# A third home for raw down blocks, the residual in DRAM, and an eighth step by seven products

## The chip, the cores and the metric

The kernel runs on one core of one Trainium2 chip. The core's engines are PE (TensorE, the matmuls), DVE (VectorE), ACT (ScalarE), POOL (GpSimd) and SP (SyncE, which only issues transfers here). Each has its own queue and works it in order; they wait for each other by semaphores. The metric is the device time of one execution in microseconds (us).

## The reference

One layer of a hybrid decoder for 256 tokens and 16 meta tokens put ahead of them, in fp32. The model is 2048 wide, the feed-forward part 5632:

```python
u = rmsnorm(h, norm_mix)
# in projection; 8 retention heads and 4 mLSTM heads, each normed and gated
mix = jnp.concatenate([ret, hm], axis=-1) @ w_out
h = h + mix
u = rmsnorm(h, norm_ffn)
up = causal_dwconv(u @ w_up, ffn_conv_w, ffn_conv_b)      # 3 taps, over the tokens
gate, val = jnp.split(up, [FFN_DIM], axis=-1)
h = h + (jax.nn.silu(gate) * val) @ w_down
h = rmsnorm(h, norm_final)
return h[:, N_META:]
```

The change concerns the last product, (silu(gate) * val) @ w_down, and the sum h that it is added to.

## The kernel before

**Numbers in two parts.** A weight block comes from DRAM as fp32 into a tile `wraw` (4 buffers). ACT casts it to `whi`, DVE subtracts to get the rest `wlo` (5 buffers each, `load_w`, L118 to L123). The left operands are held in two parts as well (`uh`/`ul`, `mh`/`ml`, `sh`/`sl`). A product is then three matmuls: whi by the high part, whi by the low part, wlo by the high part.

**Stages.** In projection and heads (to about 383 us), out projection (to 470), then twice (for each half of the 5632 columns): the up projection with convolution and gate (470 to 718, 828 to 1084), and the down projection in two passes, b=0 (the left 1024 of the 2048 output columns) and b=2 (the right 1024): 718 to 773 and 773 to 828, 1084 to 1140 and 1140 to 1198. The rest is the last norm and the output.

**A down pass** has 11 steps q, each over 256 of the inner columns, for two token tiles tt and two output blocks of 512 (j). A *plain* step does it with `product`: 24 matmuls of 128x512 (L827, L828, L830). A *fast* step (`seven`, L859 to L862) computes the 2x2 block product with seven block products in place of eight, in 21 matmuls. Its left sides (S1 to S4, A11, A12, A22) are made in the up stage. Its right sides are differences and sums of the weight blocks B11, B12, B21, B22; one of these sums is made early, in the out stage or the up stage, by `Early`: POOL loads three blocks into a home, DVE combines them in two operations, and the result is put into DRAM (`kept`). In the down step SP loads the kept sum and three raw blocks into one of two homes (`left`, in the old hT), DVE forms `ta` (L844, 128x1024) and `tb` (L845, 128x512) in wraw tiles, and each group is split by ACT and DVE (L764, L766). FAST has seven of the eleven steps; in the last pass the last two of them (BOTH) are plain.

**PSUM.** A pass uses eight banks: four `cs[tt, j]` (tile atps) and four `ps` (mmps) for the products that are shared. After the last fast step, `share` turns the four into sums and adds them to the residual; at the end of the pass ACT copies the four cs into x tiles (L951), and accumulating transfers (`onto`, L878, by POOL) add these to the residual as well. The next pass starts its matmuls on the same banks.

**The residual** h is transposed in the first up half by 32 DVE operations of 32x512 (`transposed_h`, L675) into `hn` (two token tiles by 2048) in SBUF, where all sums are added.

**The last pass.** Its order of steps is written out. The last four plain steps do only j=0 in their turn; for j=1 they follow `alone`, after the pass, first for token tile 0 in 512 columns, then for token tile 1 in two halves of 256, so that the first tile's norm and output (`finish`: L711 to L727) runs beside the second tile's matmuls. `add` (L900) adds a bank to hn, `squares` (L694) sums the squares on ACT, `gather` (L703, L704) collects them.

**Order.** A scheduler sets the order on each engine from its own model of the times, within the dependencies and the `issue_after` hints in the code.

Of the kernel before, what the change touches and what calls it, by code (L numbers as in the profile page):

```python
# [16 lines left out]
P = 128  # L17
DM = 2048
# [65 lines left out]
def trunk(ctx: ExitStack, tc: tile.TileContext, io, out: bass.AP):  # L84
# [477 lines left out]
    hnp_cm = pool("hnp", 1, side="right")  # L562
    hnp = hnp_cm.__enter__()
    hn = hnp.tile([P, 2, DM], F32, name="hn")
# [7 lines left out]
    ssq = hn[:, 0, 0:NQ]  # L572
# [20 lines left out]
    FAST = [1, 2, 3, 5, 6, 7, 8]  # L593
# [5 lines left out]
    class Early:  # L599


        def __init__(self, b, q, home, after, pace=None):

            self.home, self.age = home, 0
            self.kept = dram.tile([P, 512], F32, name=f"kept{b}_{q % NQD}", bufs=1)
# [6 lines left out]
        def finish(self, after):  # L612
            t = self.home[:, 0, :]
            with tc.issue_after(after.ins):
                nc.vector.tensor_tensor(out=t, in0=self.home[:, 1, :], in1=t, op=ALU.subtract)
            nc.vector.tensor_tensor(out=t, in0=self.home[:, 2, :], in1=t, op=ALU.add)
            nc.gpsimd.dma_start(self.kept, t)

    early, running = {}, []
    ahead = [(0, q) for q in FAST[:5]]  # L620
# [43 lines left out]
    x5 = midp.tile([P, 5, 512], F32, name="x5")  # L664
    pace = midp.tile([P, 1], F32, name="pace")

    def x_tile(i):
        return x5[:, i, :]

    def transposed_h(i, a):  # L670

        src = hT[32 * i : 32 * (i + 1), :, T0 + 2 :].rearrange("p k (t a e) -> p k t a e", t=2, e=32)
        dst = hn[32 * a : 32 * (a + 1), :, :].rearrange("p t (k f) -> p k t f", f=P)
        for t in range(2):
            nc.vector.transpose(dst[:, :, t, 32 * i : 32 * (i + 1)], src[:, :, t, a, :])  # L675

    def conv3(ps, f, name):
# [3 lines left out]
        o = wk2.tile([P, SEQ], F32, name=name)  # L681
# [59 lines left out]
    left = hT.rearrange("p k t -> p (k t)")[:, 0:4096].rearrange("p (i a n) -> i p a n", i=2, a=4)  # L741
    turn = 0

    for half in range(2):
        units = [(b, q) for b in (0, 2) for q in FAST if (half, b) != (1, 2) or q not in BOTH]
        homes = [left[0][:, 0:3, :], left[1][:, 0:3, :], x5[:, 1:4, :]]
        if half == 0:
            units = units[len(ahead):]
            begins = [2 + 4 * i for i in range(9)]
            homes = 9 * [homes[2]]  # L750
# [18 lines left out]
        for jj in range(NHF):  # L769
# [27 lines left out]
            else:  # L797
# [5 lines left out]
                nc.gpsimd.tensor_tensor(out=sums[:, S3, :], in0=e11, in1=e21, op=ALU.subtract)  # L803
# [28 lines left out]
        def seven(b, q, cs, ps, first, last, after, norm):  # L832
# [5 lines left out]
            turn = 1 - turn  # L838

            nc.sync.dma_start(raw[:, 0, :], early[b, q])  # L840
# [4 lines left out]
            nc.vector.tensor_tensor(out=tb[:, 0, :], in0=raw[:, 3, :], in1=raw[:, 0, :], op=ALU.subtract)  # L845
            copied = None
            for w, to in (
                (raw[:, 2:4, :], ((S4, cs[0, 1], False, False), (A12, cs[0, 0], False, False))),
                (raw[:, 0:2, :], ((S2, ps[2], first, last), (A11, ps[0], first, last))),
                (ta, ((S3, ps[1], first, last), (S1, ps[3], first, last))),  # L850
                (tb[:, 0:1, :], ((A22, cs[1, 0], False, False),)),
# [9 lines left out]
                for i, (m, o, _, end) in enumerate(to):  # L861
                    nc.tensor.matmul(o, sh[:, f, m, :], lo[:, i, :], start=False, stop=end)  # L862
            if norm:
# [4 lines left out]
                reached = nc.gpsimd.tensor_tensor(out=junk[:, 0:1], in0=tb[:, 0, 0:1], in1=tb[:, 0, 0:1], op=ALU.add)  # L868
# [4 lines left out]
        def block(tt, b):  # L873
            return hn[:, tt, b * 512 : (b + 1) * 512]
# [194 lines left out]
```

## Time and profile before

| | us |
|---|---|
| median of three runs (lowest, highest) | 1207.89 (1206.9, 1209.06) |
| profiled execution | 1207.7 |
| span of its profile | 1205.9 |
| busy: PE, DVE, ACT, POOL | 1194.6, 971.5, 709.5, 162.8 |
| granted clock of PE | 0.999 |

The profile is one execution. A row of a timeline gives start and duration, then engine, line, operation, what it writes and reads, how many, and in brackets the idle time ahead of it and what ended it. A group's row gives its count, the total busy time and the mean in ns, then the idle time ahead of the group. A row of a stretch gives its bounds, its length, the busy time of each engine, the granted clock, the share of the 16 DMA engines, and GB/s.

### The profile page before, as it was taken

What the parts mean: (1) busy time and instruction counts of PE and PEld (TensorE: products, weight loads), DVE (VectorE), ACT (ScalarE), POOL (GpSimd) and SP (SyncE); (2) the same over time, 40 slices, a digit from 0 to 9 for tenths busy, and PEclk for the clock granted to TensorE, in tenths of its full rate; (3) what the DMA queues carried; (4) which work ended last, traced back from release to release, by engine and by line L of the source; (5) the groups of instructions that cost most, each with busy time, mean ns of one, the idle gap of its engine ahead of it and who ended that gap; (6) DMA issues with size and microseconds to landing.
All of it is one profiled execution on the core that took longest, in us unless ns stands there. A gap on an engine that the chain in (4) does not pass through costs nothing.

```text
span 1205.9 us, 22794 instructions
## 1 busy us (share of the span) xinstructions
PE 1194.6 (99%) x8956; PEld 1151.2 (95%) x8956; DVE 971.5 (81%) x1444; ACT 709.5 (59%) x963; POOL 162.8 (14%) x223
## 2 busy tenths in 40 slices
PE   9999999999999999999999999999999999999997
PEld 9999999999999999999999998878999999998886
DVE  8968788766775966789889879897788778789897
ACT  8747656655656646555555557664555555556664
POOL 0100001111110311021122100202022112100232
PEclk9999999999999999999999999999999999999999
DMA  8765555666565965766766834959787777755956
GB/s 278 269 212 164 170 184 170 197 183 192 169 192 165 349 200 175 252 220 212 253 219 214 279 117 175 278 177 276 284 251 255 223 240 249 261 176 211 274 181 186
DMA packets 83004, 263.27 MB, mean 218 GB/s; under 512 B 14672, under 2 KB 18896, under 8 KB 82768
## 3 DMA queue, kind: packets, MB, share of 16 engines
q1 hardware_dynamic: 71952, 223.85, 57.0%
q0 software_dynamic: 10368, 37.11, 10.1%
q8 instruction: 70, 1.15, 0.4%
q10 hardware_dynamic: 576, 0.85, 0.2%
q14 instruction: 38, 0.31, 0.1%
HBM read 243.42 MB, written 11.27 MB: 211 GB/s over the span
## 4 chain that ended last, share of the span: by engine, by line
PE 96%; DMA 2%; DVE 1%; ACT 0%; issue 0%; SPq 0%; DVEq 0%; ACTq 0%
PE mmps L130 26%; PE mmps L131 25%; PE mmps L133 25%; PE atps L827 2%; PE atps L828 2%; PE atps L830 2%; PE mmps L860 2%; PE mmps L862 2%; PE mmps L859 2%; PE atps L862 1%; PE atps L860 1%; PE atps L859 1%; DMA hn<-x 1%; PE atps L379 1%; DMA hT<-in_wd 1%; PE atps L371 0%
## 5 line engine op out<-in xcount | busy, mean ns | idle before, releaser
L121 ACT CAST whi<-wraw 128x1024 fp32r<-128x1024 f32 x352 | 369.3, 1050 | 342.0 <-PE mmps L131 228.7
L123 DVE TENSOR_TENSOR wlo<-wraw,whi 128x1024 fp32r<-128x1024 f32 x352 | 432.3, 1230 | 72.5 <-ACT whi L121 70.0
L130 PE MATMUL mmps<-uh,whi 128*128 128x258 f32 x1408 | 346.1, 283 | 0.0
L131 PE MATMUL mmps<-ul,whi 128*128 128x258 f32 x1408 | 346.0, 283 | 0.0
L130 PEld LDWEIGHTS mmps<-uh,whi 128*128 128x128 f32 x1408 | 267.6, 190 | 0.1
L131 PEld LDWEIGHTS mmps<-ul,whi 128*128 128x128 f32 x1408 | 267.1, 190 | 0.1
L130 PE MATMUL mmps<-xh,whi 128*128 128x272 f32 (+2 forms) x864 | 219.8, 288 | 0.0
L131 PE MATMUL mmps<-xl,whi 128*128 128x272 f32 (+2 forms) x864 | 218.3, 286 | 0.0
L133 PE MATMUL mmps<-uh,wlo 128*128 128x258 f32 x1408 | 196.5, 282 | 0.0
L133 PEld LDWEIGHTS mmps<-uh,wlo 128*128 128x128 f32 x1408 | 179.9, 189 | 0.0
L131 PEld LDWEIGHTS mmps<-xl,whi 128*128 128x128 f32 x864 | 162.8, 188 | 0.0
L130 PEld LDWEIGHTS mmps<-xh,whi 128*128 128x128 f32 x864 | 162.5, 188 | 0.1
L133 PE MATMUL mmps<-xh,wlo 128*128 128x272 f32 (+2 forms) x864 | 126.7, 285 | 0.0
L133 PEld LDWEIGHTS mmps<-xh,wlo 128*128 128x128 f32 x864 | 114.2, 188 | 0.0
L680 DVE TENSOR_TENSOR cu<-mmps,rstd 128x258 f32<-128x258 f32 x88 | 37.4, 425 | 55.3 <-PE mmps L133 54.8
L764 ACT CAST whi<-hT 128x1024 fp32r<-128x1024 f32 x52 | 53.6, 1052 | 27.2 <-PE atps L828 7.3
L766 DVE TENSOR_TENSOR wlo<-hT,whi 128x1024 fp32r<-128x1024 f32 x52 | 62.1, 1220 | 4.9 <-ACT whi L764 3.7
L131 PE MATMUL mmps<-mixl,whi 128*128 128x258 f32 x256 | 63.0, 283 | 0.0
L130 PE MATMUL mmps<-mixh,whi 128*128 128x258 f32 x256 | 62.4, 282 | 0.0
L764 ACT CAST whi<-wraw 128x1024 fp32r<-128x1024 f32 (+1 forms) x52 | 43.0, 838 | 16.8 <-PE mmps L860 6.8
L766 DVE TENSOR_TENSOR wlo<-wraw,whi 128x1024 fp32r<-128x1024 f32 (+1 forms) x52 | 52.2, 1037 | 0.6 <-PE mmps L862 0.2
L827 PE MATMUL atps<-whi,mh 128*128 128x512 f32 (+1 forms) x132 | 50.9, 387 | 1.3 <-ACT whi L121 1.1
(280 smaller groups left out, 1700.1 us busy)
## 6 DMA issues: line engine op xcount, KB each, us to landing
wraw<-in_wu SPq DMA_DIRECT2D x176, 512.0 KB, 4.4
wraw<-in_wi SPq DMA_DIRECT2D x108, 512.0 KB, 4.1
hT<-in_wd SPq DMA_DIRECT2D x26, 768.0 KB, 4.7
wraw<-in_wd SPq DMA_DIRECT2D x36, 512.0 KB, 4.7
wraw<-in_wo SPq DMA_DIRECT2D x32, 512.0 KB, 4.2
x<-in_wd POOLq DMA_DIRECT2D x13, 768.0 KB, 7.0
hn<-x POOLq DMA_DIRECT2D x27, 256.0 KB, 7.9
hT<-kept SPq DMA_DIRECT2D x26, 256.0 KB, 2.9
```

What stands on the lines that cost most here:

```text
L121: nc.scalar.copy(hi, raw)
L123: nc.vector.tensor_tensor(out=lo, in0=raw, in1=hi.bitcast(F32), op=ALU.subtract)
L130: nc.tensor.matmul(ps, hi[:, k, :], xh(kk), start=kk == first, stop=False)
L131: nc.tensor.matmul(ps, hi[:, k, :], xl(kk), start=False, stop=False)
L133: nc.tensor.matmul(ps, lo[:, k, :], xh(kk), start=False, stop=kk == last)
L680: evacuated = nc.vector.tensor_tensor(out=u, in0=ps[:, :NQ], in1=rstd2, op=ALU.mult)
L764: copied = nc.scalar.copy(hi, x)
L766: return copied, nc.vector.tensor_tensor(out=lo, in0=x, in1=hi.bitcast(F32), op=ALU.subtract)
L827: nc.tensor.matmul(ps, ah[i], hi[:, i, cols], start=first and i == 0, stop=False)
L859: nc.tensor.matmul(o, sh[:, f, m, :], hi[:, i, :], start=begin, stop=False)
L860: nc.tensor.matmul(o, sl[:, f, m, :], hi[:, i, :], start=False, stop=False)
L862: nc.tensor.matmul(o, sh[:, f, m, :], lo[:, i, :], start=False, stop=end)
```

## The change

- FAST gets q=4: eight of eleven steps are fast. In the last pass six are (the steps 7 and 8 stay plain there), and the order of its steps becomes 0, 1, 2, 7, 3, 4, 8, 5, 6, 9, 10.
- Early keeps both of its sums (512 KB) instead of one (256 KB). A fast step then loads 512 KB of sums, 512 KB of raw blocks and 256 KB for B22 into a tile of its own (b22, two buffers), and forms only one difference (ta). The weight layout wd7 and the sign of S3 follow.
- A third home for raw blocks (`third`); the three take turns.
- The out stage makes eight sums early instead of five (four homes `eh`), the first up half eight instead of nine, the second up half fourteen instead of twelve, with four homes.
- The residual no longer stays in SBUF: it is transposed in pieces (128 operations of 32x128) into `third`, four transfers put it into DRAM (`hnd`), and the 16 accumulating transfers of half 0 add to it there. In half 1, b=0, four transfers bring it back (512 KB each, one after each of the first four fast steps), and gfin (1 MB) follows after the fifth.
- There are four x tiles instead of five; ssq lives in rstd2; vt has one buffer.

The core of the diff:

```diff
-    FAST = [1, 2, 3, 5, 6, 7, 8]
+    FAST = [1, 2, 3, 4, 5, 6, 7, 8]
...
-            self.kept = dram.tile([P, 512], F32, name=f"kept{b}_{q % NQD}", bufs=1)
+            self.kept = dram.tile([P, 2, 512], F32, name=f"kept{b}_{q % NQD}", bufs=1)
...
-    homes = 2 * [eh.tile([P, 3, 512], F32, name=f"eh{i}") for i in range(3)]
-    begins = [1, 4, 6, 8, 10]
+    homes = 2 * [eh.tile([P, 3, 512], F32, name=f"eh{i}") for i in range(4)]
+    begins = [0, 2, 3, 5, 7, 8, 10, 12]
...
-    def transposed_h(i, a):
...
+    def transposed_h(g, i):
+        turned = left[2][:, 2 * (g % 2) : 2 * (g % 2) + 2, :]
...
+        for a in range(4):
+            dst = turned[32 * a : 32 * (a + 1), :, :].rearrange("p t (k f) -> p k t f", f=P)
+            for t in range(2):
+                nc.vector.transpose(dst[:, :, t, 32 * i : 32 * (i + 1)], src[:, :, t, a, :])
+        if i == 3:
+            nc.gpsimd.dma_start(hnd[:, :, 512 * g : 512 * (g + 1)], turned)
...
+    left = [left[0], left[1], midp.tile([P, 4, 512], F32, name="third")]
...
             raw = left[turn]
-            turn = 1 - turn
-            nc.sync.dma_start(raw[:, 0, :], early[b, q])
-            nc.sync.dma_start(raw[:, 1:4, :], io["wd7"][b // 2, half * NQD + q][:, 1:4, :])
-            ta, tb = (wpool.tile([P, 2, 512], F32, name="wraw", bufs=4) for _ in range(2))
-            nc.vector.tensor_tensor(out=ta, in0=raw[:, 0:1, :].to_broadcast([P, 2, 512]), in1=raw[:, 1:3, :], op=ALU.subtract)
-            nc.vector.tensor_tensor(out=tb[:, 0, :], in0=raw[:, 3, :], in1=raw[:, 0, :], op=ALU.subtract)
+            turn = (turn + 1) % 3
+            w = io["wd7"][b // 2, half * NQD + q]
+            nc.sync.dma_start(raw[:, 0:2, :], early[b, q])
+            nc.sync.dma_start(raw[:, 2:4, :], w[:, 2:4, :])
+            b22 = midp.tile([P, 1, 512], F32, name="b22", bufs=2)
+            nc.sync.dma_start(b22[:, 0, :], w[:, 1, :])
+            ta = wpool.tile([P, 2, 512], F32, name="wraw", bufs=4)
+            nc.vector.tensor_tensor(out=ta, in0=raw[:, 2:4, :], in1=raw[:, 1:2, :].to_broadcast([P, 2, 512]), op=ALU.subtract)
...
+            if half == 1 and b == 0 and fast.index(q) < 5:
+                refill(fast.index(q), copied)
...
         def block(tt, b):
-            return hn[:, tt, b * 512 : (b + 1) * 512]
+            return (hn if half == 1 else hnd)[:, tt, b * 512 : (b + 1) * 512]
...
-            steps = [0, 1, 4, 2, 7, 3, 5, 6, 8, 9, 10] if final else range(NQD)
+            steps = [0, 1, 2, 7, 3, 4, 8, 5, 6, 9, 10] if final else range(NQD)
...
-                        x = x_tile((4, 3, 1, 0)[2 * j + n])
+                        x = x_tile((3, 1, 0, 2)[2 * j + n])
```

Where the order moves. On SP, at the start of half 0, b=2, the loads before the change are these (kept and hT: the two loads of a fast step; wraw x4: the plain steps' weights):

```order
L840 DMA hT<-kept_1_6644 128x512
L841 DMA hT<-in_wd 128x1536
L118 DMA wraw<-in_wd 128x1024 x2
L840 DMA hT<-kept_2_6936 128x512
L841 DMA hT<-in_wd 128x1536
L118 DMA wraw<-in_wd 128x1024 x4
L840 DMA hT<-kept_3_7228 128x512
L841 DMA hT<-in_wd 128x1536
```

And the same place after it (b_: the tile b22):

```order
L118 DMA wraw<-in_wd 128x1024
L845 DMA third<-in_wd 128x1024
L844 DMA third<-kept_1_6082 128x1024
L847 DMA b_9494<-in_wd 128x512
L118 DMA wraw<-in_wd 128x1024
L845 DMA hT<-in_wd 128x1024
L844 DMA hT<-kept_2_6372 128x1024
L847 DMA b_9670<-in_wd 128x512
L118 DMA wraw<-in_wd 128x1024
L845 DMA hT<-in_wd 128x1024
L844 DMA hT<-kept_3_6676 128x1024
L847 DMA b_9713<-in_wd 128x512
```

Three transfers stand for a fast step where two stood, and the loads of step 3 are issued ahead of the last plain weights instead of behind them. On DVE, at the end of the program, before:

```order
L900 TENSOR_TENSOR hn<-atps,hn 128x512 x2
L703 TENSOR_REDUCE rest<-ss_5848 128x1
L704 TENSOR_SCALAR rest<-rest 128x1
L900 TENSOR_TENSOR hn<-atps,hn 128x512
L711 TENSOR_SCALAR frt<-ss_5848,rest 128x1
L900 TENSOR_TENSOR hn<-atps,hn 128x256
L713 SCALAR_TENSOR_TENSOR frt<-frt,fr_5852 128x1
L714 SCALAR_TENSOR_TENSOR frt<-frt,fr_5852 128x1
L723 TENSOR_SCALAR hn<-hn,frt 128x256
L723 TENSOR_SCALAR hn<-hn,frt 128x768
L721 SCALAR_TENSOR_TENSOR hn<-hn,frt,gfin 128x512
```

And after (the lines are shifted: L907 is `add`, L725 and L723 the scalings of `finish`, L705 and L706 `gather`):

```order
L907 TENSOR_TENSOR hn<-atps,hn 128x512
L706 TENSOR_SCALAR rest<-rest 128x1
L907 TENSOR_TENSOR hn<-atps,hn 128x512
L713 TENSOR_SCALAR frt<-ss_5861,rest 128x1
L715 SCALAR_TENSOR_TENSOR frt<-frt,fr_5865 128x1
L716 SCALAR_TENSOR_TENSOR frt<-frt,fr_5865 128x1
L725 TENSOR_SCALAR hn<-hn,frt 128x256
L725 TENSOR_SCALAR hn<-hn,frt 128x768
L723 SCALAR_TENSOR_TENSOR hn<-hn,frt,gfin 128x512
L907 TENSOR_TENSOR hn<-atps,hn 128x256
L705 TENSOR_REDUCE rest<-ss_5861 128x1
L706 TENSOR_SCALAR rest<-rest 128x1
```

The first sum of 256 columns has moved from ahead of the three scalings to behind them. On PE, the wide matmuls of token tile 0 that follow alone now all stand ahead of the narrow ones of token tile 1; before, the last pair stood among them.

More of the change, by code (lines that the diff above doesn't have):

```diff
@@ L904, in trunk, with refill @@
             up_cm.__exit__(None, None, None)
[L905 removed]
+            more_cm = pool("more", 1, side="right")
             more = more_cm.__enter__()
+            hn = more.tile([P, 2, DM], F32, name="hn", bufs=1)
             gfin = more.tile([P, DM], F32, name="gfin", bufs=1)
[L908 removed]
+            def refill(n, after):
+                cols = slice(n * 512, (n + 1) * 512)
+                with tc.issue_after(after.ins):
+                    if n < 4:
+                        nc.gpsimd.dma_start(hn[:, :, cols], hnd[:, :, cols])
+                    else:
+                        nc.gpsimd.dma_start(gfin, io["gfin"])
             junk = more.tile([P, 512], F32, name="junk", bufs=1)
```

50 lines of the change are left out of this document (21 added, 29 removed).

## The prediction

> **What bounds the kernel now.** I read the page's busy shares first, then the list of what PE (TensorE) waits for, then the four down passes as stretches of time.
>
> ```profile
> span 1205.9 us, 22794 instructions
> PE 1194.6 (99%) x8956; PEld 1151.2 (95%) x8956; DVE 971.5 (81%) x1444; ACT 709.5 (59%) x963; POOL 162.8 (14%) x223
> PE 96%; DMA 2%; DVE 1%; ACT 0%; issue 0%; SPq 0%; DVEq 0%; ACTq 0%
> ```
>
> PE works 1194.6 of 1205.9 us and is 96% of the chain that ended last. A change pays by taking matmuls away or by closing a PE gap; everything on another engine is free as long as PE's next operand is there. The gaps are few:
>
> ```profile
> PE atps L827 <- ACT whi L121: 1.1, 2, 0.7
> PE atps L130 <- ACT whi L224: 0.7, 1, 0.7
> PE atps L827 <- ACT x L951: 0.2, 1, 0.2
> ```
>
> (total us, times, longest). The L827 rows lie in the down passes, the other at the start, untouched. The down passes, in order (half 0 b=0, b=2, half 1 b=0, b=2), then two short stretches:
>
> ```profile
> core 0: us, PE busy (x) PEld busy (x) DVE busy (x) ACT busy (x) POOL busy (x), PEclk, DMA share, GB/s
> 718.00:773.00 55.00, 55.00 (x243) 45.17 (x242) 49.88 (x54) 33.00 (x38) 3.54 (x4) 1.00 0.66 222
> 773.00:828.00 55.00, 53.90 (x234) 43.55 (x234) 50.44 (x52) 34.62 (x41) 6.99 (x8) 1.00 0.69 203
> 1084.50:1140.00 55.50, 55.50 (x243) 45.24 (x241) 50.35 (x55) 34.66 (x40) 4.03 (x5) 1.00 0.73 244
> 1140.00:1197.70 57.70, 57.54 (x274) 47.99 (x273) 52.62 (x58) 36.73 (x54) 19.26 (x18) 1.00 0.61 184
> 1122.00:1128.00 6.00, 6.00 (x28) 4.91 (x27) 5.32 (x6) 2.91 (x4) 0.00 (x0) 1.00 1.03 370
> 410.00:415.00 5.00, 5.00 (x44) 5.00 (x44) 5.00 (x6) 2.25 (x3) 2.67 (x4) 1.00 1.03 412
> ```
>
> PE is full in each pass but the second, which lacks 1.1 us. DVE (VectorE) is over 90% busy there, and the transfers come in bursts: 370 and 412 GB/s are the most that full queues moved.
>
> **Part 1: one more step by seven products.** In four passes one step (4 in three of them; in the last pass six fast steps instead of five) needs 21 matmuls of 128x512 instead of 24: 4 x 3 = 12 fewer. PE starts one every 0.23 us:
>
> ```profile
> 765.73 0.39 PE L828 MATMUL atps<-whi,ml 128*128 128x512 f32 x1
> 765.96 0.39 PE L827 MATMUL atps<-whi,mh 128*128 128x512 f32 x1
> 766.19 0.39 PE L828 MATMUL atps<-whi,ml 128*128 128x512 f32 x1
> ```
>
> 12 x 0.23 = **-2.76 us**, wholly on the path, since PE is the path. A plain step is 24 x 0.23 = 5.5 us, a fast one 21 x 0.23 = 4.8 us.
>
> **Part 2: third home, one wraw tile per fast step.** The two L827 waits:
>
> ```profile
> 793.62 0.50 PE L827 MATMUL atps<-whi,mh 128*128 128x512 f32 x1 [0.45 <-ACT whi L121]
> 819.27 0.51 PE L827 MATMUL atps<-whi,mh 128*128 128x512 f32 x1 [0.65 <-ACT whi L121]
> 788.90 0.93 SPq L118 DMA_DIRECT2D wraw<-in_wd  x2
> 792.52 1.05 ACT L121 CAST whi<-wraw 128x1024 fp32r<-128x1024 f32 x1 [2.94 <-DMA wraw<-in_wd]
> SPq L840 <- DVE wlo L766: 63.4, 11, 13.8
> ```
>
> The weights of plain step 4 are issued only at 788.90, the cast (792.52) waits 2.94 us for them, and PE waits for the cast. SP issues in order: its hT loads wait for a free home (63.4 us in the two passes of half 0), and the four wraw slots hold both differences of each fast step. With three homes, one difference per step, and step 4 no longer plain, both causes shrink. I take both waits as gone: **-1.1 us** (bounds 0 and -1.1).
>
> On DVE the second difference falls away:
>
> ```profile
> L675 DVE STREAM_TRANSPOSE hn<-hT 32x512 f32<-32x512 f32 x32 | 20.7, 681 | 0.2
> L845 DVE TENSOR_TENSOR wraw<-hT 128x512 f32<-128x512 f32 x26 | 17.8, 685 | 0.1
> L336 DVE STREAM_TRANSPOSE turns<-vT 128x256 f32<-128x256 f32 x16 | 7.0, 437 | 0.0
> L337 DVE STREAM_TRANSPOSE turns<-vT 128x32 f32<-128x32 f32 x16 | 2.7, 169 | 0.0
> ```
>
> 26 x 0.685 = 17.8 us less, none of it on the path: DVE stays behind PE in cover. But a fast step still asks DVE for about 5.1 us (today's split and differences, 5.8, less 0.685) against PE's 4.8, so eight in a row eat about 8 x 0.3 = 2.4 us of DVE's lead. The plain steps 9, 10 and 0 give it back, so I price this at nothing.
>
> **Part 3: residual by DRAM.** The 32 transposes become 128 of 32x128. No row shows that shape; by the 128x32 and 128x256 rows one costs 0.17 to 0.44 us, by a straight line 0.28: 128 x 0.28 = 36 us against 20.7, so +15 us (+1 to +35). They run in the first up half, where this row gives the cover:
>
> ```profile
> 475.00:700.00 225.00, 225.00 (x1879) 225.00 (x1878) 192.78 (x295) 122.93 (x165) 39.22 (x55) 1.00 0.71 233
> ```
>
> DVE has 32 us free: nothing on the path; at the upper end 3 us could show. The eight sums of the out stage (five before) bring three loads and larger stores there; that stage had PE full at 412 GB/s, so I price it at 0, with 2 us as the upper bound.
>
> The 16 accumulating transfers of half 0 go to DRAM. Their nearest rows are the same transfers into SBUF:
>
> ```profile
> hn<-x POOLq DMA_DIRECT2D x27, 256.0 KB, 7.9
> 766.03 2.77 POOL L878 DMA_DIRECT2D hn<-x  x3 [1.25 <-DVE x L887]
> 772.92 2.25 ACT L951 COPY x<-atps 128x512 f32<-128x512 f32 x4
> 777.87 0.39 PE L827 MATMUL atps<-whi,mh 128*128 128x512 f32 x1
> ```
>
> The last of the three is issued near 767.6 and lands, by the median of 7.9 us, at 775.5. With one x tile fewer, the fourth copy out of PSUM at the pass boundary now waits for exactly that landing. PE wants this bank at 777.87, the copy takes 0.57: slack 1.8 us. At SBUF's speed this costs nothing; if DRAM takes longer by more than 1.8 us, PE waits. For all new waits together (this landing, a late load) I take one late load of the size seen, **+0.65 us** (0 to +4).
>
> **Part 4: the end.** In the last stretch the scaling of the first token tile now stands on DVE ahead of the first half-block sum, and the third of the four sums of a wide bank (L907 now, L900 before) waits for the last accumulating transfer.
>
> ```profile
> 1180.49 1.05 ACT L121 CAST whi<-wraw 128x1024 fp32r<-128x1024 f32 x1 [2.75 <-DMA wraw<-in_wd]
> 1191.39 0.28 PE L827 MATMUL atps<-whi,a21h 128*128 128x256 f32 x1
> 1192.22 0.63 PE L830 MATMUL atps<-wlo,mh 128*128 128x512 f32 x2
> 1197.30 0.40 PE L830 MATMUL atps<-wlo,mh 128*128 128x256 f32 x2
> 1192.89 0.69 DVE L900 TENSOR_TENSOR hn<-atps,hn 128x512 f32<-128x512 f32 x1 [0.51 <-PE atps L830]
> 1194.88 0.42 DVE L900 TENSOR_TENSOR hn<-atps,hn 128x256 f32<-128x256 f32 x1 [0.24 <-PE atps L830]
> 1195.67 1.43 DVE L723 TENSOR_SCALAR hn<-hn,frt 128x256 f32<-128x256 f32 x2
> 1197.67 0.14 DVE L703 TENSOR_REDUCE rest<-ss 128x1 f32<-128x4 f32 x1
> 1197.92 0.41 DVE L900 TENSOR_TENSOR hn<-atps,hn 128x256 f32<-128x256 f32 x1
> 1198.91 0.21 DVE L711 TENSOR_SCALAR frt<-ss,rest 128x1 f32<-128x1 f32 x1 [0.58 <-ACT junk L694]
> ```
>
> E is PE's end (1197.30 + 0.40 = 1197.70). Today seven narrow matmuls (1191.39 to 1192.22, 0.83 us) stand ahead of the last pair of 512; now all 48 narrow ones follow it, so the sum of 1192.89 can come 0.83 us earlier against E. The three scalings take 1195.67 to 1197.67: 2.00 us. At best they now run from E-2.86 to E-0.86; the first half-sum follows, its square is in 0.99 us later (as 1197.92 to 1198.91), reduce and scale take 0.25 (1197.67 to 1197.92), and the second half-sum starts at E+0.38 instead of E+0.22: +0.16 us. But the last fast step now ends 12 wide matmuls nearer to E (57 before, 45 after), so its sums and their transfers end up to 2.76 us nearer to E, unless the 2.75 us that ACT lost at 1180.49 to a late load come back, which would cancel it. Bounds +0.16 and 0.16 + 2.76 = +2.9; I take **+0.8**, near the lower, because that load is now issued earlier.
>
> **Sum:** -2.76 - 1.10 + 0.65 + 0.80 = -2.4 us. The profiled execution took 1207.7: 1207.7 - 2.4 = 1205.3. It lies 0.2 below the median of the runs, 1207.89, so on that footing 1205.5, a change of -0.2%. Some 0.2% (2.4 us) is about what a measurement of this kernel can tell from no change; the forecast stands on that edge.
>
> **Refill traffic against full queues.** In half 1 b=0 each of five fast steps now asks for 1280 KB of weights and sums (1.31 MB) and four of them for 512 KB of residual as well: 1.83 MB in 4.8 us is 382 GB/s. The rows above show 370 and 412 at full queues, so the four steps need 0.0 to 0.7 us more than PE gives them in all (4 x 1.83 / 370 = 19.8 us against 19.2), which a lookahead of one home, 4.8 us, covers. In the Trainium skill, "DMA: Bandwidth & Descriptors", section "Where 436 GB/s comes from", the HBM side (about 358 GB/s) binds for transfers between HBM and SBUF; by it the steps would need 4 x 1.83 / 358 = 20.4 us, an estimate that adds 0.6 us to the shortage. The trace does not agree: 412 GB/s passed here.
>
> **The rivals.**
> *Everything arrives* (0.25): both waits go, the end costs 0.16 and no new wait comes: 1207.7 - 3.7 = 1204.0, on the median's footing 1204.2. For it: PE waited only 1.3 us in four passes. Against it: lead on DVE shrinks in eight fast steps in a row.
> *The end comes late* (0.18): the last accumulating transfer lands after the last pair of 512, and the end costs the whole 2.9: -2.76 - 1.10 + 0.65 + 2.9 = -0.3, 1207.6. For it: median 7.9 us of such a transfer; against it: few transfers are left there. It decides from about 2 us of lateness.
> *Transfers become the bound* (0.14, slower): the refill and gfin (1 MB in the fifth step: 2.36 MB, 6.4 us at 370 against 4.8, 1.6 us short, 2.2 with the four before) meet the last up half's stores, the lookahead is empty at the start of half 1 b=0, and the two waits stay: in that pass 2.2, and as much where 16 transfers into DRAM crowd the loads of each of the two passes of half 0: 3 x 2.2 = 6.6; -2.76 + 0.8 + 6.6 = +4.6, on the median's footing 1212.5; where only half of the 6.6 shows, 1209.2. For it: 0.73 DMA share in that pass already. Against it: a third home of lookahead. It decides where less than 2.2 us of loads lie ahead of PE.
> *DRAM sums land late* (0.08, slower): at twice 7.9 us the bank at 777.87 is copied 6.1 us late (7.9 - 1.8): 1205.5 + 6.1 = 1211.6. Nothing in the trace shows such a transfer.
>
> **How the numbers follow.** The forecast itself holds 0.35, from 1204.7 to 1206.8 by its two open terms. Faster by over 0.2% (below 1205.5): the first rival and half of the forecast, 0.25 + 0.18 = 0.43. Within 0.2%: the other half and the late end, 0.17 + 0.18 = 0.35. Slower: 0.14 + 0.08 = 0.22, of which the half-shown case lies within 0.2%, so 0.19, and same 0.38. The range runs from 1203.6 (the first rival with 0.6 us of unlisted gain from DVE's shorter steps) to 1210.0, above the half-shown transfer bound; what lies beyond is the DRAM case and the full transfer bound.
>
> **What would show it.** In the profile after: about 12 fewer matmuls of 128x512, L845's successor for the second difference absent, no PE wait of 0.4 us for a wraw cast in half 0 b=2; transposes near 0.28 us; no PE wait for an x copy at the boundary of half 0; in half 1 b=0 PE full at a DMA share near 0.85. At the end, the time from the last matmul to the last scaling says what part 4 cost. A PE wait for a cast of a hT or third tile, or for an x copy, of over 1 us makes the forecast wrong.

## The result, and the profile after

| | before | after |
|---|---|---|
| median of four runs each (lowest, highest), us | 1207.39 (1206.84, 1209.06) | 1218.12 (1217.78, 1220.54) |
| profiled execution, and its span | 1207.7, 1205.9 | 1217.8, 1216.0 |
| PE's end, and from there to the end of the span | 1197.70, 8.2 | 1205.38, 10.6 |

The ratio is 1.0091 [1.0073, 1.0108]: the kernel became slower, by about 11 us, and the forecast of 1205.5 (range to 1210.0) was wrong. The page's busy shares after:

```profile
span 1216.0 us, 23007 instructions
PE 1195.9 (98%) x8944; PEld 1150.1 (95%) x8944; DVE 980.7 (81%) x1536; ACT 710.8 (58%) x973; POOL 186.2 (15%) x248
```

The twelve matmuls are gone (8956 to 8944 records), yet PE is busy 1.3 us longer. PE's waits after (total us, times, longest):

```profile
PE mmps L867 <- DVE wlo L769: 7.1, 4, 4.7
...
PE mmps L130 <- DVE hT L576: 0.5, 1, 0.5
...
PE atps L833 <- DVE wlo L123: 0.2, 1, 0.2
```

The two waits for a `wraw` cast of before are gone. In their place PE waits four times, inside fast steps (L867), for DVE's `wlo`. The passes in the prediction's order (half 0 b=0, b=2, half 1 b=0), then the start of the third and the stretch behind its longest wait:

```profile
core 0: us, PE busy (x) PEld busy (x) DVE busy (x) ACT busy (x) POOL busy (x), PEclk, DMA share, GB/s
718.00:773.00 55.00, 55.00 (x246) 45.30 (x245) 48.48 (x51) 35.45 (x40) 3.53 (x4) 1.00 0.77 251
773.00:828.00 55.00, 53.07 (x229) 42.25 (x229) 46.95 (x47) 36.99 (x42) 4.44 (x6) 1.00 0.78 223
1084.00:1140.00 56.00, 50.80 (x213) 40.39 (x213) 45.83 (x48) 33.12 (x38) 4.29 (x6) 0.94 0.82 291
1084.00:1100.00 16.00, 15.59 (x72) 12.61 (x71) 13.13 (x16) 9.28 (x12) 0.00 (x0) 1.00 0.47 148
1117.20:1122.00 4.80, 4.80 (x11) 3.40 (x12) 4.52 (x5) 4.06 (x6) 0.00 (x0) 0.50 1.00 386
```

Half 0 b=0 is still full. Half 0 b=2 lacks 1.9 us, half 1 b=0, which was full, 5.2. DVE is busy less in these two than in the same passes before (46.95 and 45.83 against 50.44 and 50.35): it stands idle for 8 to 10 us of each. What it waits for the timeline shows, first in half 0 b=2:

```profile
786.29 1.23 DVE L850 TENSOR_TENSOR wraw<-third 128x1024 f32<-128x1024 f32 x1 [2.94 <-DMA third<-kept]
787.43 1.22 DVE L769 TENSOR_TENSOR wlo<-hT,whi 128x1024 fp32r<-128x1024 f32 x1
788.70 0.74 PE L867 MATMUL mmps<-wlo,sh 128*128 128x512 f32 x2 [0.83 <-DVE wlo L769]
```

L850 is `ta`. DVE works in order, and the scheduler has put the `ta` of a later step (its raw blocks are in `third`) ahead of a split of the step that PE is in (from `hT`). The later step's kept sums land late, DVE stands still 2.94 us for them, and PE waits for the split behind. The long wait of half 1 b=0 has the same form, and late loads are added to it (POOL, then SP, DVE, ACT, PE):

```profile
1100.95 2.86 POOL L921 DMA_DIRECT2D hn<-hnd  x4 [21.78 <-PE atps L867]
1103.81 0.55 POOL L923 DMA_DIRECT2D gfin<-in_gfin  x1
1105.09 0.33 SPq L844 DMA_DIRECT2D hT<-kept  x1
1105.69 0.33 SPq L847 DMA_DIRECT2D b<-in_wd  x1
1114.70 1.22 DVE L850 TENSOR_TENSOR wraw<-hT 128x1024 f32<-128x1024 f32 x1 [3.90 <-DMA hT<-kept]
1115.85 2.35 DVE L769 TENSOR_TENSOR wlo<-third,whi 128x1024 fp32r<-128x1024 f32 x2
1117.57 0.62 ACT L767 CAST whi<-b 128x512 fp32r<-128x512 f32 x1 [8.51 <-DMA b<-in_wd]
1117.12 0.80 PE L867 MATMUL mmps<-wlo,sh 128*128 128x512 f32 x1 [4.71 <-DVE wlo L769]
```

The refill does not go out "one after each of the first four fast steps": `issue_after` only gives an order. POOL stood 21.78 us for a wait and then issued all four and gfin, 3.1 MB, between 1100.95 and 1104.36. SP's loads that were issued behind that landed late. The 512 KB of kept sums issued at 1105.09 let the `ta` of their step start only at 1114.70 (9.6 us; the median of this transfer is 4.5), and the split of the step that PE was in (from `third`, 1115.85) stood behind that `ta`: PE waited 4.71 us for it, until 1117.12. The 256 KB of b22, issued at 1105.69, were there for ACT's cast only at 1117.57 (11.8 us; median 3.7); PE's first matmul with it starts at 1118.24, as the cast ends, so without the wait for the split PE would soon have stood for this cast. The next matmuls started at half rate:

```profile
1120.54 0.63 PE L865 MATMUL mmps<-whi,sl 128*128 128x512 f32 x1
1120.97 0.63 PE L864 MATMUL atps<-whi,sh 128*128 128x512 f32 x1
1121.39 0.63 PE L865 MATMUL atps<-whi,sl 128*128 128x512 f32 x1
```

0.43 us apart instead of 0.23, at a granted clock of 0.50: 11 intervals from 1117.12 took 5.03 us instead of 2.53, another 2.5 us lost.

The sum against before, on the spans: matmuls -2.76; waits 7.1 + 0.2 + 0.5 less the 1.1 + 0.2 that went and 0.3 less at the start, +6.2; half clock +2.5; end +2.4; together +8.3 of +10.1. The other 1.8 us are not placed.

### The profile page after: what moved, and what is told of

It is laid out like the page before. It is cut to its first block, busy times and chain, and to the rows that moved or that the text cites. A ratio compares the mean times of both kernels' runs of the same rounds, so it can differ in the third digit from the quotient of the medians.

```text
span 1216.0 us, 23007 instructions
## 1 busy us (share of the span) xinstructions
PE 1195.9 (98%) x8944; PEld 1150.1 (95%) x8944; DVE 980.7 (81%) x1536; ACT 710.8 (58%) x973; POOL 186.2 (15%) x248
## 5 line engine op out<-in xcount | busy, mean ns | idle before, releaser
L121 ACT CAST whi<-wraw 128x1024 fp32r<-128x1024 f32 x344 | 357.6, 1046 | 232.8 <-PE mmps L131 130.3
L123 DVE TENSOR_TENSOR wlo<-wraw,whi 128x1024 fp32r<-128x1024 f32 x344 | 423.3, 1234 | 60.1 <-ACT whi L121 58.0
L867 PE MATMUL mmps<-wlo,sh 128*128 128x512 f32 x120 | 43.4, 403 | 7.1 <-DVE wlo L769 7.1
L769 DVE TENSOR_TENSOR wlo<-hT,whi 128x1024 fp32r<-128x1024 f32 x40 | 47.9, 1219 | 1.6 <-ACT whi L767 1.5
L686 DVE SCALAR_TENSOR_TENSOR gt<-cu,par,gt 128x256 f32<-128x256 f32 x88 | 42.8, 487 | 7.7 <-ACT gt L684 6.4
L130 PEld LDWEIGHTS mmps<-mixh,whi 128*128 128x128 f32 x256 | 48.3, 190 | 0.7 <-DVE hT L576 0.7
L767 ACT CAST whi<-hT 128x1024 fp32r<-128x1024 f32 x40 | 41.2, 1051 | 13.1 <-DMA hT<-in_wd 3.0
L131 PEld LDWEIGHTS mmps<-mixl,whi 128*128 128x128 f32 x256 | 48.4, 189 | 0.0
```

The source lines that it names most:

```text
L121: nc.scalar.copy(hi, raw)
L123: nc.vector.tensor_tensor(out=lo, in0=raw, in1=hi.bitcast(F32), op=ALU.subtract)
L130: nc.tensor.matmul(ps, hi[:, k, :], xh(kk), start=kk == first, stop=False)
L131: nc.tensor.matmul(ps, hi[:, k, :], xl(kk), start=False, stop=False)
L686: nc.vector.scalar_tensor_tensor(out=o, in0=u[:, j : j + SEQ], scalar=pcol("fw", 3 * f + j), in1=o, op0=ALU.mult, op1=ALU.add)
L767: copied = nc.scalar.copy(hi, x)
```

## The experiments

The theories before the first runs: (A) the refill in one burst makes the loads of half 1 b=0 late; (B) `ta` stands too early in DVE's order and blocks PE's splits; (C) eight fast steps in a row use more than loads and DVE supply, so that there is no lead left to stand anything.

### First: spread the burst, move `ta`, mend the end

e1_paced lets POOL read `ta` of the third to seventh fast step, and the refill follow it:

```diff
-            if half == 1 and b == 0 and fast.index(q) < 5:
-                refill(fast.index(q), copied)
+            if half == 1 and b == 0 and 2 <= fast.index(q) < 7:
+                refill(fast.index(q) - 2, nc.gpsimd.tensor_tensor(out=pace, in0=ta[:, 0, 0:1], ...))
```

> The changed kernel with one edit: in half 1, b=0, the four transfers that bring the residual back and gfin are each held by a small POOL operation that reads ta of the fast steps 3 to 7, so that they can't all start at once. Theory A (burst): in the changed kernel all five were issued within 3.6 us, 3.1 MB, and delayed the weight loads behind them to 9.5 to 11.8 us; spread out, the PE wait of 4.71 us and the half clock after it go, the time falls by 6 to 8 us, to 1210 to 1212. Rival B (total traffic): the pass asks for more than the queues move in any order; then the wait is only split up, PE still waits 3 to 5 us in that pass, and the time stays at 1215 to 1218.

Measured: 1224.99, 1.0133 [1.0116, 1.0150]. The one long wait is gone, but five waits for `wlo` (longest 2.3) sum to 6.3, and late loads cost another 2.6 us in a cast of b22 and 2.6 us in casts of plain weights. `ta` is formed well ahead of PE, so the transfers may have been held less than meant; SP's loads in the stretch from 1105 to 1150 had medians of 6.3 to 9.6 us to landing. Spreading alone does not save the time.

e2_ta_late holds `ta` behind the first two splits of its own step:

```diff
+                if w is b22:
+                    with tc.issue_after(parted.ins):
+                        nc.vector.tensor_tensor(out=ta, ...)
```

> The changed kernel with one edit: the difference ta of a fast step stands on DVE behind the first two splits of its own step, instead of up to two steps earlier, where DVE waited for its load while PE waited for the split queued behind it. Theory C (order on DVE): the waits of 0.83, 1.10 and 0.48 us go, and some of the 4.71 us, since the splits queued behind that ta no longer wait for it: 1213 to 1216. Rival B (the loads themselves are late): the same splits wait for their own loads, and the time stays within 1 us of 1218.

Measured: 1241.54, 1.0269 [1.0253, 1.0284]; PE waits for the splits of `ta` itself (L869) 16 times, 8.0 us in all. That is too late: it says nothing on (B). e3_both is both edits, e4_tail adds e8's edit (below) to them.

> Both edits, the paced return of the residual and the late ta. If A and C are both right and separate, PE waits in the down passes fall below 0.5 us and the time is that of the prediction plus the late end: 1207 to 1208.5. If total traffic binds (B), a wait of over 2 us stays in half 1, b=0, and the time is over 1210.

> Both edits and a third: the sum of token tile 1's wide bank, which waits for the last accumulating transfer, stands behind token tile 0's last sum on DVE instead of ahead of it. In the changed kernel 0.76 us of DVE waiting stood there, and the time from PE's end to the end of the span was 10.6 us against 8.2 before. Theory D (order at the end): the end costs 1 to 2 us less than in the run with two edits, and the time is 1205.5 to 1207. Rival: the transfer is late for the second token tile as well, and nothing is won, within 0.5 us of the run with two edits.

Measured: 1245.40, 1.0303 [1.0287, 1.0318] and 1244.09, 1.0299 [1.0276, 1.0321]. Both carry e2's loss and tell nothing more.

### Second: without the refill; early sums, gfin and end by themselves

e5_zero leaves the residual and half 0's sums out of the output: hn is set to zero by POOL in place of the 2 MB of transfers.

```diff
-                        nc.gpsimd.dma_start(hn[:, :, cols], hnd[:, :, cols])
+                        nc.gpsimd.memset(hn[:, :, cols], 0.0)
```

> The changed kernel with the 2 MB that bring the residual back left out: POOL sets hn to zero instead, so the residual and half 0's down products are missing from the sum; gfin (1 MB) is still loaded there. Theory B' (the returned residual is what half 1, b=0, has no room for): loads behind it land in 4 to 6 us instead of 9.5 to 11.8, the PE wait of 4.71 us and the half clock go, 1209.5 to 1212. Rival E (lookahead is empty at the start of the pass, since the last early sums hold the homes): the transfers were only the last straw, a wait of over 2 us stays in that pass, 1214 to 1217.

Measured: 1220.95, 1.0100 [1.0080, 1.0121]. Nothing is won in all. The wait of 4 to 5 us near 1117 to 1121, which after, e8 and e9 have, is gone here; but PE still waits 7 times, 7.6 us, for `wlo` in fast steps (two of these waits, 2.4 us, in the last pass), and half 1 b=0 still lacks 3.8 us:

```profile
1084.00:1140.00 56.00, 52.23 (x217) 40.87 (x216) 49.72 (x56) 35.31 (x42) 5.00 (x6) 0.97 0.75 254
1089.77 1.23 DVE L850 TENSOR_TENSOR wraw<-hT 128x1024 f32<-128x1024 f32 x1 [2.05 <-DMA hT<-kept]
1090.91 1.22 DVE L850 TENSOR_TENSOR wraw<-third 128x1024 f32<-128x1024 f32 x1
1092.05 1.22 DVE L850 TENSOR_TENSOR wraw<-hT 128x1024 f32<-128x1024 f32 x1
1093.18 1.22 DVE L769 TENSOR_TENSOR wlo<-hT,whi 128x1024 fp32r<-128x1024 f32 x1
1094.46 0.74 PE L867 MATMUL mmps<-wlo,sh 128*128 128x512 f32 x2 [2.24 <-DVE wlo L769]
```

This wait begins at 1092, where after the change no refill had been issued yet. So (A) alone falls: the loss doesn't need the burst. The rows above it show (B) again: three `ta` stand in a row on DVE, the first waits 2.05 us for its kept sums, and the split that PE needs comes behind the third. e1 (2.31 us at 1096), e8 and e9 have the same three ahead of the same split.

e6_begins starts the early sums of the second up half sooner (34 in place of 38), e9_gfin loads gfin in the last pass, e8_tail puts token tile 1's wide sum, which waits for the last accumulating transfer, behind token tile 0's last sum on DVE:

```diff
-begins = [2 + 38 * i // (len(units) - 1) ...]
+begins = [2 + 34 * i // (len(units) - 1) ...]
```

> The changed kernel with the early sums of the last up half spread over 34 instead of 38 of its 44 projections, so that the last of them frees its home four projections (some 20 us) sooner. Theory E: the first fast steps' loads are then issued before the pass starts, the queues no longer idle from 1084 to 1100 us (148 GB/s there, 255 before), PE waits in that pass fall by more than half, 1210 to 1214. Theory B': the 3.1 MB come at the same time on top of the same loads, and the time stays at 1217 to 1219.

```diff
-            if half == 1 and b == 0 and fast.index(q) < 5:
+            if half == 1 and b == 0 and fast.index(q) < 4:
...
+            if half == 1 and b == 2 and q == 2:
+                refill(4, nc.gpsimd.tensor_tensor(out=pace, in0=ta[:, 0, 0:1], ...))
```

> The changed kernel with gfin's 1 MB loaded in the last pass, behind ta of its second fast step, instead of in half 1, b=0. If every MB in that burst costs alike (B'), a third of the PE wait of 4.71 us goes and with it the half clock: 1213 to 1216; if the residual's 2 MB are enough to empty the lookahead, over 3 us of waiting stay there and the time is 1216.5 to 1218.5.

```diff
+            with tc.issue_after(summed.ins):
-            add(cs[1, 1], 1, c)
+                add(cs[1, 1], 1, c)
```

> The changed kernel with one edit: token tile 1's wide sum, which waits for the last accumulating transfer, stands behind token tile 0's last sum on DVE instead of ahead of it. Theory D: 0.7 to 1.5 us less at the end, 1216.6 to 1217.4, and the time from PE's end to the end of the span falls from 10.6 to about 9.5 us. Rival: the first half-sum still stands behind the three scalings, which set the end, and nothing is won (1218).

Measured: e6 1223.13, 1.0116 [1.0101, 1.0131], with waits of 3.22 at 1098 and 4.03 at 1117; e9 1221.46, 1.0097 [1.0071, 1.0122], with waits of 2.31 and 4.41; e8 1221.61, 1.0108 [1.0090, 1.0127], its end 9.3 us (span 1218.2, PE's end 1208.95) against 10.6, the waits in the passes not fewer (9.7 us for `wlo`). None of the three is the cause; the order at the end is worth about 1 us.

### Third: the eighth step taken away, and put in alone

e7_seven makes step 4 plain again in every pass (five fast steps in the last one, as before) and keeps the rest: DRAM, refill burst, third home, both sums. With the step go its early sums: six in the first up half instead of eight, twelve in the second instead of fourteen.

```diff
-    FAST = [1, 2, 3, 4, 5, 6, 7, 8]
+    FAST = [1, 2, 3, 5, 6, 7, 8]
...
-            steps = [0, 1, 2, 7, 3, 4, 8, 5, 6, 9, 10] if final else range(NQD)
+            steps = [0, 1, 4, 2, 7, 3, 5, 6, 8, 9, 10] if final else range(NQD)
```

> The changed kernel with step 4 plain again (seven of eleven by seven products, the old order of the last pass, eight early sums in the out stage of which the last is for b=2); third home, both sums kept and residual in DRAM stay. If the eighth fast step is what empties DVE's and the queues' lead, the waits in the down passes fall below 3 us and the time is 1.000 to 1.005 of the kernel before. If the loads of the other parts do it, it stays over 1.007: 12 matmuls more (+2.8 us) and fewer waits cancel.

b1_eight is the kernel before with step 4 fast and no more than the room for it (four x tiles, vt with one buffer, eleven early sums in the first up half):

```diff
-    FAST = [1, 2, 3, 5, 6, 7, 8]
+    FAST = [1, 2, 3, 4, 5, 6, 7, 8]
...
-            begins = [2 + 4 * i for i in range(9)]
+            begins = [2 + 39 * i // 10 for i in range(11)]
```

> The kernel before with step 4 by seven products and nothing else of the change but what makes room for it (four x tiles, one vt buffer): two homes, one sum kept, residual in SBUF, eleven early sums in the first up half. 12 matmuls fewer are worth 2.8 us. Theory H: DVE's 5.8 us for each of eight fast steps in a row against PE's 4.8 use up a lead of about 4 us and then cost PE 2 to 4 us in three passes: 1.002 to 1.008 of the kernel before. Rival: the plain steps refill the lead and the gain comes: 0.997 to 0.999.

Measured: e7 1208.92, 0.9999 [0.9983, 1.0016], the same as before; b1 1226.30, 1.0148 [1.0121, 1.0175], slower than the whole change. Half 1 b=0 of e7, then of b1, and two of the largest rows of b1's PE waits:

```profile
1084.00:1140.00 56.00, 56.00 (x260) 46.56 (x259) 46.99 (x51) 36.20 (x42) 6.91 (x9) 1.00 0.88 298
```

```profile
1084.00:1140.00 56.00, 50.74 (x224) 39.21 (x223) 51.61 (x62) 33.63 (x41) 1.10 (x2) 0.97 0.52 181
```

```profile
PE atps L827 <- ACT whi L121: 5.4, 6, 1.6
PE atps L859 <- ACT whi L764: 2.0, 2, 1.4
```

With seven fast steps PE is full through the same burst of 3.1 MB; with eight, and no refill at all, it lacks 5.3 us. So the loss comes with the eighth step and its early sums, and the rest of the change makes it smaller, not larger (1.0091 against 1.0148). How it costs, these two don't say: in b1, which has two homes and a second difference on DVE, PE waits mostly for casts, and 1.9 us of its waits are for x copies, which the four x tiles can make.

e7 settles two terms besides. Its longest PE wait is the one that the prediction named for the DRAM sums, an x copy at the pass boundary:

```profile
PE atps L830 <- ACT x L967: 2.1, 1, 2.1
781.61 0.59 ACT L967 COPY x<-atps 128x512 f32<-128x512 f32 x1 [4.16 <-DMA hnd<-x]
```

It fits four x tiles rather than slow DRAM: the 16 transfers took a median of 7.9 us in e7 and 7.3 after, into SBUF 7.9 before, and b1, with four x tiles and the residual in SBUF, waits for x copies too. And its end has after's order on DVE (scalings, then the half-sums) with five fast steps in the last pass:

```profile
1198.00 0.88 DVE L725 TENSOR_SCALAR hn<-hn,frt 128x256 f32<-128x256 f32 x2
1199.46 0.42 DVE L907 TENSOR_TENSOR hn<-atps,hn 128x256 f32<-128x256 f32 x1
1200.71 0.42 DVE L907 TENSOR_TENSOR hn<-atps,hn 128x256 f32<-128x256 f32 x1
```

PE ends at 1200.45, so the second half-sum starts at E+0.26 (before: E+0.22), and the end takes 8.2 us (span 1208.7) as before. So the 2.4 us at the end come with the sixth fast step of the last pass and its order of steps.

e11_ta_own puts `ta` behind the last split of the step before it, e10_onesum goes back to one kept sum and a `tb` per fast step:

```diff
+            with tc.issue_after(parted_last.ins) if parted_last else nullcontext():
-            nc.vector.tensor_tensor(out=ta, ...)
+                nc.vector.tensor_tensor(out=ta, ...)
```

> The changed kernel with one edit: the difference ta of a fast step stands on DVE at the start of its own step, behind the last split of the step before, instead of one to two steps ahead. Theory C (order on DVE, as it should have been tried the first time): a ta whose load is late then holds up only its own step, the waits at 788.7, 810.7 and 1100.1 us go and the long one shrinks: 1.003 to 1.007 of the kernel before. Rival F (the loads are late whatever the order): 1.008 to 1.011.

```diff
-            self.kept = dram.tile([P, 2, 512], F32, ...)
+            self.kept = dram.tile([P, 512], F32, ...)
...
+            ta, tb = (wpool.tile([P, 2, 512], F32, name="wraw", bufs=4) for _ in range(2))
```

> The changed kernel with the old fast step in it: one early sum is kept and loaded (1024 KB for a fast step instead of 1280, 256 KB to store instead of 512), and DVE forms the second difference again (0.685 us); eight fast steps, third home and residual in DRAM stay. Theory G (traffic: 256 KB more for each fast step and each store is what makes the loads late): 1.002 to 1.006 of the kernel before. Rival H (DVE): 5.8 us on DVE against 4.8 on PE in eight steps in a row costs PE 2 to 3 us a pass more: 1.010 to 1.018.

Measured: e11 1218.52, 1.0083 [1.0068, 1.0098]; e10 1231.03, 1.0185 [1.0158, 1.0213]. In e11 half 0 b=2 is full (773 to 828: 55.00), so there `ta`'s place is the cause (B). It is full with eight fast steps in a row, so in half 0 the row alone costs nothing, and (C) falls there. Half 1 b=0 keeps a wait of 3.8 us, now for the cast of a b22 that was issued behind the burst:

```profile
1111.94 0.62 ACT L768 CAST whi<-b 128x512 fp32r<-128x512 f32 x1 [6.58 <-DMA b<-in_wd]
1112.61 0.80 PE L866 MATMUL atps<-whi,sh 128*128 128x512 f32 x1 [3.76 <-ACT whi L768]
```

e10 says that the second kept sum is a help: without it the loss is 1.9% in place of 0.9 to 1.2%.

### Fourth: one plain step into the row of eight

a2_after_again is the changed kernel, unedited, on the same chip as the three runs beside it. c2_plain7 makes step 7 plain in half 1 b=0 alone and puts it in the middle of the row:

```diff
-            steps = [0, 1, 2, 7, 3, 4, 8, 5, 6, 9, 10] if final else range(NQD)
+            steps = [0, 1, 2, 7, 3, 4, 8, 5, 6, 9, 10] if final else [0, 1, 2, 3, 7, 4, 5, 6, 8, 9, 10] if half == 1 else range(NQD)
```

> The changed kernel again, unedited, as a mark for the runs beside it: earlier runs of edits that leave the passes alone came out at 1.010 to 1.011 of the kernel before, where the changed kernel had 1.009. Expected 1.008 to 1.011, with the waits of half 1, b=0, of 5 us or more.

> The changed kernel with one pass changed: in half 1, b=0, step 7 is plain and stands after step 3, so that three and four fast steps follow each other instead of eight; 3 matmuls more, one early sum fewer, and the residual still comes back there in one burst. Theory I (eight fast steps in a row, not the returned residual): PE's waits in that pass fall below 1 us, nothing of the half clock is left, 1.001 to 1.004 of the kernel before. Rival B' (the burst): a wait of over 2 us stays there, 1.006 to 1.010.

Measured: a2 1222.35, 1.0117 [1.0102, 1.0132]; c2 1213.44, 1.0043 [1.0029, 1.0057]. Half 1 b=0 of a2 and then of c2:

```profile
1084.00:1140.00 56.00, 47.56 (x201) 36.78 (x200) 47.78 (x54) 34.18 (x41) 3.40 (x5) 0.97 0.76 271
```

```profile
1084.00:1140.00 56.00, 56.00 (x259) 46.51 (x258) 49.43 (x52) 36.34 (x41) 7.09 (x10) 1.00 0.92 314
```

Three matmuls more (0.7 us) and the pass is full again, with the burst in it, and the median is 8.9 us below a2's. One early sum fewer (13 instead of 14) goes with it, and the up half's last `cu` on DVE came at 1087.33 instead of 1094.84 (a2; before, with twelve, 1084.45). So the row of eight and the fourteenth early sum, which could both eat DVE's lead, are not told apart: in half 1 (C) is borne out only for the two together. Half 0 b=2 of c2, where `ta` is not moved, lacks 3.8 us.

c1_plain7_ta is c2 with e11's edit; c5_mid0_ta also moves plain step 0 behind step 4 in half 0 (and the flag that opens a bank with it):

> The same with ta at the start of its own step as well. In the run with that edit alone no wait was left in half 0. Theory I and C together: no wait over 0.6 us in the three passes that are not the last, and with 9 matmuls fewer than before (-2.1 us) 0.998 to 1.002. Rival: the last pass, which waited 2.6 us in the run with ta alone, waits on: 1.001 to 1.004.

```diff
+                                       else [1, 2, 3, 4, 0, 5, 6, 7, 8, 9, 10]
```

> The same, and in both passes of half 0 the plain step 0 stands after step 4: the same work, four and four fast steps in a row instead of eight. Theory I: DVE's lead and the loads are refilled in the middle, no wait in half 0, no worse than the run without it and up to 1 us better. Rival J: step 1 now comes first in each pass, its loads and the four bank copies stand in its way, and each pass of half 0 waits 1 to 3 us at its start: 2 to 5 us slower than the run without it.

Measured: c1 1214.30, 1.0051 [1.0036, 1.0066]; c5 1220.30, 1.0099 [1.0084, 1.0114]. c1 fills half 0 b=2 (55.00) as e11 did, but meets the burst:

```profile
1107.72 1.04 ACT L121 CAST whi<-wraw 128x1024 fp32r<-128x1024 f32 x1 [10.34 <-DMA wraw<-in_wd]
1108.81 0.79 PE L831 MATMUL atps<-whi,sh 128*128 128x512 f32 x1 [5.73 <-ACT whi L121]
```

Now the plain step's own weights, issued behind the refill, are late. In c5 a pass that begins with a fast step lacks its operands at once (2.7 us at 777), and 6.7 us at 1114 remain.

### Fifth: `ta`, the refill and the plain step together

c6_spread is c1 with the refill held by POOL to the second to fifth fast step, and gfin in the last pass; c7_spread_noord is c6 without e11's edit.

```diff
+            k = 4 if (half, b, q) == (1, 2, 2) else fast.index(q) - 1 if half == 1 and b == 0 else -1
+            if 0 <= k < 4 or (half, b, q) == (1, 2, 2):
+                refill(k, nc.gpsimd.tensor_tensor(out=pace, in0=ta[:, 0, 0:1], ...))
```

> The run with step 7 plain in half 1, b=0, and ta at the start of its own step, with the return of the residual spread: each of its four transfers is held by a POOL operation that reads ta of the second to fifth fast step, and gfin follows in the last pass, behind ta of its second fast step. In the run without the spread one wait was left, 5.7 us for the weights of step 7, which landed 14 us after their issue behind the five transfers, and about 2 us of half clock after it. If that burst was their cause, both go and the time is 0.996 to 0.999 of the kernel before (9 matmuls fewer are 2.1 us, the two waits of before 1.1). Rival B (total traffic): the wait moves to a later step or to the last pass, 1.001 to 1.005.

> The same without the edit of ta's place: in the run with step 7 plain alone the burst cost no wait, but half 0, b=2, waited 3.2 us for splits queued behind an early ta, and 1.1 us for a copy. Theory C: these stay, 1.001 to 1.004 of the kernel before. Rival: the scheduler's order comes out otherwise and they go, below 1.000.

Measured: c6 1209.64, 1.0015 [0.9998, 1.0032], within the measurement of before; c7 1214.95, 1.0057 [1.0037, 1.0076]. Half 0 b=2 and half 1 b=0 of c6:

```profile
773.00:828.00 55.00, 55.00 (x237) 44.57 (x236) 49.63 (x50) 36.54 (x43) 6.07 (x7) 1.00 0.81 239
1084.00:1140.00 56.00, 56.00 (x246) 45.98 (x245) 47.98 (x49) 35.41 (x40) 10.54 (x14) 1.00 0.84 284
```

No wait is left in these two, nor in the first pass. With nine matmuls fewer than before (2.1 us) and the 1.3 us of old waits gone, PE should end 3.4 us earlier than before; it ends at 1197.89, 0.2 us later. About 1.4 us of small waits stand in the last pass, 2.2 us are not placed. The end takes 10.0 us (span 1207.9) against 8.2. Without `ta`'s place (c7) 5 us come back, 2.4 of them in half 0 b=2, 2.3 at 1158.9 in the last pass. No version ran faster than the kernel before. The one that is missing has eight fast steps in half 1 b=0 with `ta` moved and the refill spread: whether the row costs anything there by itself is not shown.

## Why the prediction was wrong, point by point

- **Part 1, -2.76 us: right.** 8956 to 8944 records, still 0.23 us each at full clock.
- **Part 2, the two waits gone, -1.1: right** (they are gone in e7 as well, where step 4 is plain). **"Eight in a row eat about 2.4 us of DVE's lead … so I price this at nothing": the step that failed.** I set the later plain steps 9, 10 and 0 against the row and never asked how large the lead is inside it; and I counted DVE's work, 5.1 us a step against PE's 4.8. The runs show that the eighth step with its early sums brings the loss (e7, without them: 0.9999; b1, with little else: 1.0148), but not by DVE's work: DVE stood idle 8 to 10 us in each of the two passes, 4.1 and 8.4 us of that in front of a `ta` whose kept sums had not landed, with the splits queued behind it. The term of the sum for all new waits, +0.65 (0 to +4), measured 7.8 us (7.1 + 0.2 + 0.5), and 2.5 us of half clock came on top, for which the sum had no term. The mark that I had named was a PE wait of over 1 us for a cast of a hT or `third` tile; the profile has two of over 1 us (1.10 and 4.71), for the other half of the split, DVE's `wlo`. Why a plain step in the row helps in half 1 (c2) is argued, not shown: it takes 5.5 us of PE against 4.8 and its weights lie in tiles of their own, so three homes get time to fill.
- **Refill, "which a lookahead of one home, 4.8 us, covers": failed too, in second place.** I spread 1.83 MB evenly over each step; it came as 3.1 MB at once, with loads 9.6 and 11.8 us under way behind it. That made the wait of 4.71 us and its half clock, together with `ta`'s place: e5, without 2 MB of it, has no such wait, and e11, with `ta` moved, still has 3.8 us of one. Where lead was left (e7, c2) the burst cost nothing; in c1 it cost 5.7 us and the clock, and c6 took that away. A rate was the wrong measure: the time of one late load against the lead is the right one.
- **An order on DVE that I had not looked at.** A `ta` waiting for data ahead of a split: c7 against c6, 0.4% (5.3 us); e11 fills half 0 b=2. The prediction asked what is queued behind a new wait only for ACT's copies.
- **Part 3: right.** Transposes were priced at 0.28 us and took 0.281, the first up half stayed full. DRAM sums were not slower than the same transfers into SBUF before (7.3 us against 7.9), and that rival fell:

```profile
L675 DVE STREAM_TRANSPOSE third<-hT 32x128 f32<-32x128 f32 x128 | 31.8, 281 | 0.8
hnd<-x POOLq DMA_DIRECT2D x16, 256.0 KB, 7.3
```

- **Part 4, +0.8: the mechanism right, the size off.** It cost 2.4, inside 0.16 to 2.9. E is 1204.98 + 0.40 = 1205.38; the second half-sum starts 1.94 us behind it instead of 0.22:

```profile
1204.98 0.40 PE L833 MATMUL atps<-wlo,mh 128*128 128x256 f32 x2
...
1201.40 0.69 DVE L907 TENSOR_TENSOR hn<-atps,hn 128x512 f32<-128x512 f32 x1 [0.76 <-DMA hn<-x]
...
1206.07 0.41 DVE L907 TENSOR_TENSOR hn<-atps,hn 128x256 f32<-128x256 f32 x1
1207.32 0.42 DVE L907 TENSOR_TENSOR hn<-atps,hn 128x256 f32<-128x256 f32 x1
```

  As its upper bound argued, the last accumulating transfer is late (0.76 us of DVE); e8, which takes that wait out of the way, gives 1.3 us of the 2.4 back, and e7, with five fast steps, ends as before. Of the chances, the "end comes late" case was the better reading.
- **The rival "transfers become the bound"** was nearest in place (half 0, half 1 b=0), with 6.6 us for the waits against 7.1. But its reason was the rate, and e5, without 2 MB of it, is as slow.

Still open: whether eight fast steps in a row cost anything in half 1 b=0 once `ta` is moved and the refill spread; whether it is there the row or the fourteenth early sum that takes the lead (no run has the one without the other); why the first kept sums of that pass land late in e1, e5, e8 and e9 (they are issued late, as a home that an early sum still holds would have it, but e6, with its early sums sooner, waits 3.22 us as well); the waits of c6 in its last pass and the 2.2 us there; the 1.8 us of the sum.

## What to carry to other kernels

On each engine that works in order, ask which operation that waits for data stands ahead of one that the bound needs now; a helper engine can be idle for 8 us of a pass and still hold up the bound. When a step is made cheaper for the engine that bounds, ask what loads and helper engines need for one such step, and set that against the lead inside the row of such steps, not against the average of the pass. Price a burst by how long one load behind it takes to land, and look whether an ordering hint really holds it back.

## What the hardware showed that I had not expected

A long PE wait costs twice: behind 4.71 us of idling (after) the matmuls ran 0.43 us apart for 5 us, behind 2.24 us (e5) again:

```profile
1095.83 0.63 PE L867 MATMUL atps<-wlo,sh 128*128 128x512 f32 x1
1096.25 0.63 PE L864 MATMUL mmps<-whi,sh 128*128 128x512 f32 x1
1096.68 0.63 PE L865 MATMUL mmps<-whi,sl 128*128 128x512 f32 x1
```

From 700 us on, over the twenty profiles of this study, it followed all 13 gaps of 3.0 us or more, 8 of 13 between 1.8 and 2.7, and 2 of 17 between 1.2 and 1.65. So the length alone doesn't decide it below 3 us, and a wait of that size may cost 2 us more. The Trainium skill, "TensorE: Matmul & The Clock Gate", Part 1, has the clock halved after an idle window of about 3.4 us in a free-running count; the gap of 4.71 us agrees, the one of 2.24 us is shorter than that rule asks for.
